# Sums of the second feed-forward's weights formed during the mixer and kept in DRAM

## The chip, the core and the metric

The kernel runs on one core of one Trainium2 chip. A core has TensorE (matmuls; PE in the profile, its weight loads PEld), VectorE (DVE), ScalarE (ACT), GpSimd (POOL) and SyncE (SP), which here only issues transfers. Transfers run on 16 DMA engines; each issuing engine has its queues, and SP's and POOL's carry nearly all bytes here. The metric is the device time of one execution in microseconds; lower is better.

## The reference, cut to what matters

One decoder layer for 256 tokens of width 2048 in float32: a feed-forward, a mixer (sliding-window attention beside an RWKV-7 recurrence, both gated), a cross-attention into 256 memory rows, a second feed-forward and a last norm.

```
def swiglu(h, w_gate, w_up, w_down):
    return (jax.nn.silu(h @ w_gate) * (h @ w_up)) @ w_down

x = x + 0.5 * swiglu(rms_norm(x, ffn1_norm), ffn1_w_gate, ffn1_w_up, ffn1_w_down)
x = gated_parallel_mixer(x, ...)        # w_in, w_proj_attn, w_proj_rwkv, w_out
x = memory_cross_attention(x, mem, ...) # w_cross_q, w_cross_kv, w_cross_o
x = x + 0.5 * swiglu(rms_norm(x, ffn2_norm), ffn2_w_gate, ffn2_w_up, ffn2_w_down)
return rms_norm(x, final_norm)
```

Each feed-forward has gate and up of 2048 x 5632 and a down of 5632 x 2048.

## The kernel before, in words

**Precision.** Each float32 operand is split into two fp32r parts, hi (a rounding, cast by ScalarE, L339) and lo (the rest, a subtraction on VectorE, L340). A product is three matmuls into one accumulator, xhi by hi, xhi by lo and xlo by hi (`times`, L413 to L415), each 128 x 128 by 128 x 512.

**Weights.** All weights stream from DRAM once, in the order of `weight_plan`. A unit is two chunks of 128 rows by 512 columns (KU = 2; 512 KB). `load` issues it on SP's queue into a ring: in the feed-forwards two units as one transfer of 1 MB into "raw2" (4 buffers of 1 MB), otherwise 512 KB into "raw" (4 buffers). `split_unit` makes hi and lo, in rings of three. `next_item` hands the next unit (or pair of units) to the products and keeps loads four units ahead and splits two units ahead. SP takes its transfers in order: a load that waits for its buffer holds all behind it. In the mixer a unit serves both blocks of 128 tokens: 12 matmuls.

**The feed-forward.** Its 11 blocks of 512 columns come in groups of 4, 4 and 3 (`GROUPS`). Block 0 takes gate and up one after the other by plain `product`; blocks 1 to 10 take them together by `product_pair`, over 8 chunk pairs q: two chunks of rows of both gate and up, with the two blocks of tokens. After each group comes a part of down, by `product_pair` too (but for the last two quarters of the last group).

**Pairs in seven.** A chunk pair is a product of a 2 x 2 block matrix of inputs by one of weights: eight products (24 matmuls). For the q in `SEVEN` it takes seven (21 matmuls) by Winograd's form of Strassen's scheme, p1 to p7, from sums of the input blocks (`combinations`, made once for all column blocks, in the feed-forward's beginning) and sums of the weight blocks. The weight sums are formed in place by `sums`: four VectorE subtractions of 128 x 512 (L350 to L353) from the raw gate and up rows into two "raw" buffers, then two casts (thi, L355) and two rests (tlo, L356) into one buffer each of four chunks. p1 to p7 stand in the order p1, p2, p7, p6, p4, p3, p5. Four accumulators of the scheme are finished at the last pair in seven of a block (`first` after p1, `middle` after p5). Gate and up have `SEVEN` = (0, 2, 4), so that a plain pair stands between two pairs in seven; down has (2, 4, 6) or (2, 4).

**The mixer and what fills it.** The plain products of the mixer run as a list, and small work is put between their units by `bg` (`Interleave`): groups of Python generators, one step at each tick; a tick is called after each row block of a unit, so two to a unit. A group has a limit of generators that run at once. `idle(n)` lets n ticks pass, and `bg.seen` holds the names of events. The attention stage has a loop n = 0 to 3 over the attention's gate columns and `w_proj_attn` (L1088); the RWKV part has `substitute` (31 steps of a triangular solve on VectorE) and a chain of small matmuls for each pair of heads; then come `w_proj_rwkv`, `w_out`, the cross-attention's weights, and the second feed-forward. POOL's queue moves rows that are put off to DRAM and fetched again (x1d, md, gl, ml, mem).

**What sets the order.** The program is written engine by engine in this interleaved order; a scheduler then orders each engine's instructions by what is ready, within what the buffers allow, so the built order may differ from the written one. `issue_after` puts an instruction behind another one.

## Time and profile before

| | us |
|---|---|
| median of three runs | 2270.05 (2268.65 to 2270.73) |
| the profiled execution | 2267.66 |
| its span | 2265.9 |
| first feed-forward, about | 0 to 730 |
| mixer and cross-attention, about | 730 to 1556 |
| second feed-forward, about | 1556 to 2253 |

The span is the time from the first to the last instruction of the profiled execution; the difference to its time, 1.8 us, lies around it. A row of a group of instructions gives the line, the engine, the operation, output<-inputs, partitions x elements and type, count, then busy microseconds, mean nanoseconds of one, and the idle time just before them with what ended it. A row of the timeline gives start, duration, engine, line and operation, and in brackets the idle time before it and what ended that. A row of windows gives the stretch, its length, the busy time and count of each engine, the granted TensorE clock (1.00 is full), the DMA engines' busy share and GB/s. A row of transfers gives output<-input, queue, count, KB each and the median time from issue to landing; the names of rings ("raw", "hi", "acc") are the tags above. Matmuls overlap, so their durations add up to more than the time that they take.

### The profile page before, as it was taken

Reading aid. Unit: us, or ns where it says so; the run is one execution under the profiler, and the core shown is the slowest. Engines: PE = TensorE matmul, PEld = TensorE weight load, DVE = VectorE, ACT = ScalarE, POOL = GpSimd, SP = SyncE. Lnnn points to the kernel's source line nnn. Section 1 sums busy time; section 2 is a strip of 40 time slices with the busy share of each in tenths; the row PEclk is TensorE's granted clock in tenths of the full one; section 3 lists DMA queues with packets and bytes.
Section 4 is the critical chain, followed back from the end, with each engine's and each line's share of the span. In section 5 each row is a group of like instructions: output and inputs, shape, how many; then the busy total and the mean of one; then the engine's idle time right before and its main releaser. Section 6 shows DMA issues by size and latency. Waiting matters only on the chain.

```text
span 2265.9 us, 28100 instructions
## 1 busy us (share of the span) xinstructions
PE 2244.2 (99%) x10613; PEld 1840.5 (81%) x10613; DVE 1784.2 (79%) x2283; ACT 1230.7 (54%) x1655; POOL 134.1 (6%) x194
## 2 busy tenths in 40 slices
PE   9999999999999999999999999999999999999998
PEld 7888888888888877788888888888888888888886
DVE  7899989898988477895444556547899998998987
ACT  6555555555556477544444446556555555555554
POOL 1000000000001000201220021001000000000001
PEclk9999999999999999999999999999999999999999
DMA  7565565555556544676533486657555556556563
GB/s 262 186 206 200 189 212 196 186 204 205 187 195 203 164 134 140 195 229 208 150 88 93 154 262 228 195 168 262 202 187 205 203 198 210 186 188 220 186 212 141
DMA packets 219240, 432.75 MB, mean 191 GB/s; under 512 B 14140, under 2 KB 16417, under 8 KB 219105
## 3 DMA queue, kind: packets, MB, share of 16 engines
q1 hardware_dynamic: 210432, 404.78, 54.1%
q0 software_dynamic: 8208, 25.39, 3.5%
q8 instruction: 83, 1.36, 0.2%
q10 hardware_dynamic: 464, 0.79, 0.1%
q14 instruction: 53, 0.43, 0.1%
HBM read 417.56 MB, written 13.11 MB: 190 GB/s over the span
## 4 chain that ended last, share of the span: by engine, by line
PE 86%; DVE 5%; issue 4%; DMA 2%; ACT 2%; POOL 0%; SPq 0%; POOLq 0%; DVEq 0%; ACTq 0%
PE acc L413 17%; PE acc L414 17%; PE acc L415 17%; PE mm L414 7%; PE mm L415 7%; PE mm L413 7%; DVE lo L340 2%; PE tr L600 2%; PE tr L414 2%; PE tr L415 2%; PE tr L413 2%; PE mm L1212 1%; DMA raw<-in_ffn_w_down_dram 1%; PE tr L1181 1%; ACT hi L339 1%
## 5 line engine op out<-in xcount | busy, mean ns | idle before, releaser
L339 ACT CAST hi<-raw 128x1024 fp32r<-128x1024 f32 (+1 forms) x770 | 766.0, 997 | 731.1 <-PE acc L415 423.8
L340 DVE TENSOR_TENSOR lo<-raw,hi 128x1024 fp32r<-128x1024 f32 (+1 forms) x770 | 892.2, 1164 | 341.5 <-ACT hi L339 339.5
L413 PE MATMUL acc<-hi,xhi 128*128 128x512 f32 (+1 forms) x1196 | 476.9, 399 | 3.1 <-ACT xhi L627 2.5
L414 PE MATMUL acc<-lo,xhi 128*128 128x512 f32 (+1 forms) x1196 | 465.8, 389 | 2.2 <-DVE lo L340 2.0
L415 PE MATMUL acc<-hi,xlo 128*128 128x512 f32 (+1 forms) x1196 | 464.6, 389 | 0.0
L413 PEld LDWEIGHTS acc<-hi,xhi 128*128 128x128 f32 x1196 | 224.7, 188 | 52.5 <-issue 5.1
L414 PEld LDWEIGHTS acc<-lo,xhi 128*128 128x128 f32 x1196 | 224.9, 188 | 49.9 <-DVE lo L340 4.4
L415 PEld LDWEIGHTS acc<-hi,xlo 128*128 128x128 f32 x1196 | 224.4, 188 | 47.6 <-DVE xlo L628 1.0
L355 ACT CAST thi<-raw 128x1024 fp32r<-128x1024 f32 x172 | 180.4, 1051 | 102.3 <-DVE raw L351 55.1
L356 DVE TENSOR_TENSOR tlo<-raw,thi 128x1024 fp32r<-128x1024 f32 x172 | 208.9, 1221 | 4.5 <-ACT thi L355 4.5
L413 PE MATMUL mm<-hi,xhi 128*128 128x512 f32 x380 | 149.2, 393 | 0.0
L415 PE MATMUL mm<-hi,xlo 128*128 128x512 f32 x380 | 148.1, 390 | 0.0
L414 PE MATMUL mm<-lo,xhi 128*128 128x512 f32 x380 | 148.1, 390 | 0.0
L414 PE MATMUL acc<-lo,hhi 128*128 128x512 f32 x372 | 145.5, 391 | 0.4 <-DVE lo L340 0.4
L415 PE MATMUL acc<-hi,hlo 128*128 128x512 f32 x372 | 145.4, 391 | 0.0
L413 PE MATMUL acc<-hi,hhi 128*128 128x512 f32 x372 | 145.1, 390 | 0.0
L415 PEld LDWEIGHTS mm<-hi,xlo 128*128 128x128 f32 x380 | 71.3, 188 | 15.0
L413 PEld LDWEIGHTS mm<-hi,xhi 128*128 128x128 f32 x380 | 71.4, 188 | 14.5
L414 PEld LDWEIGHTS mm<-lo,xhi 128*128 128x128 f32 x380 | 71.4, 188 | 14.5
L414 PEld LDWEIGHTS acc<-lo,hhi 128*128 128x128 f32 x372 | 69.9, 188 | 14.9 <-DVE lo L340 0.8
L350 DVE TENSOR_TENSOR raw<-raw,raw 128x512 f32<-128x512 f32 x86 | 59.1, 688 | 28.9 <-DMA raw<-in_ffn_w_up_dram 23.7
L413 PEld LDWEIGHTS acc<-hi,hhi 128*128 128x128 f32 x372 | 69.8, 188 | 14.4
(386 smaller groups left out, 3559.1 us busy)
## 6 DMA issues: line engine op xcount, KB each, us to landing
raw<-in_ffn_w_up_dram SPq DMA_DIRECT2D x88, 1024.0 KB, 6.8
raw<-in_ffn_w_down_dram SPq DMA_DIRECT2D x88, 1024.0 KB, 5.5
raw<-in_ffn_w_gate_dram SPq DMA_DIRECT2D x84, 1024.0 KB, 5.3
raw<-in_w_in_dram SPq DMA_DIRECT2D x136, 512.0 KB, 3.8
raw<-in_w_out_dram SPq DMA_DIRECT2D x32, 512.0 KB, 4.7
raw<-in_w_proj_attn_dram SPq DMA_DIRECT2D x16, 512.0 KB, 3.6
raw<-in_w_proj_rwkv_dram SPq DMA_DIRECT2D x16, 512.0 KB, 5.7
raw<-in_w_cross_kv_dram SPq DMA_DIRECT2D x16, 512.0 KB, 3.7
```

Source lines behind the costliest of these rows:

```text
L339: at["hi"] = act.copy(hi[:, s], raw[:, s])
L340: at["lo"] = dve.tensor_tensor(lo[:, s], raw[:, s], f32(hi[:, s]), ALU.subtract)
L350: dve.tensor_tensor(ta[:, 0], ru[:, 0], rg[:, 0], ALU.subtract)
L355: act.copy(hi[:, 2 * i : 2 * i + 2], t[:])
L356: dve.tensor_tensor(lo[:, 2 * i : 2 * i + 2], t[:], f32(hi[:, 2 * i : 2 * i + 2]), ALU.subtract)
L413: pe.matmul(o, xh, hi, start=first, stop=False, **how)
L414: pe.matmul(o, xh, lo, start=False, stop=False, **how)
L415: pe.matmul(o, xl, hi, start=False, stop=last, **how)
L600: pe.transpose(b[:, o : o + P], tok[:, t, col : col + P], ident[:])
L1181: pe.matmul(b[e][:, m * P : (m + 1) * P], x1[r, j, cs_], x2[r, j, cs_], start=True, stop=True,)
L1212: pe.matmul(vb[:, o : o + P][:, r], lhs(e), rhs[:, r], start=first and e == 0, stop=True, **ek,)
```

## The change

Only the second feed-forward (`last`) gets other pairs: gate and up take seven products for q = 0 to 4 (`SEVEN_2`), down for q = 2 and 4 (`SEVEN_DOWN_2`); the first keeps its pairs. Of the five, the weight sums of q = 0, 1, 3 and 4 (`STAGED`) in ten column blocks, 40 items, are not formed in place. A generator `stage`, spawned in a bg group of its own at the mixer's beginning, forms them: it loads gate's and up's two chunks (512 KB each, SP's queue) into one tile "stage" of four chunks, lets four ticks pass, subtracts four times on VectorE, and stores the tile (1 MB, SP's queue) to `sums_d` in DRAM. Six items are made early; the rest after the event "stage", at n = 2 of the loop over the attention's gates.

In the second feed-forward `load_sums` reads the sums of a staged item in two transfers of 512 KB into the ring "raw", issued on SP's queue after the weight loads; the up weights' first chunk of such a pair, which only the sums need, is not loaded any more (`first_unused`). q = 2 still forms its sums in place.

Two things change in both feed-forwards. The buffers thi and tlo of four chunks become thia, tloa, thib and tlob of two, one of each, with other sums together in a half. And the order of the seven products is p7, p6, p1, p2, p3, p4, p5: the sums' products come first.

```diff
 GROUPS = ((0, 4), (4, 4), (8, 3))
 N4 = 20
+STAGE_EARLY = 6
 AHEAD, LOADED = 2, 4
 SEVEN, SEVEN_DOWN = (0, 2, 4), ((2, 4, 6), (2, 4))
+SEVEN_2, SEVEN_DOWN_2 = (0, 1, 2, 3, 4), ((2, 4), (2, 4))
+STAGED = (0, 1, 3, 4)
 class Act:
@@ -85,13 +90,14 @@
                 for w in (wg, wu):
                     yield w, 0, KD, 0, 512
             else:
-                yield (wg, wu), 0, KD, (j * 512, j * 512), SEVEN
-        yield (wd, wd), 4 * j0, 4 * nj, (0, 512), SEVEN_DOWN[nj < 4]
+                yield (wg, wu), 0, KD, (j * 512, j * 512), SEVEN_2 if last else SEVEN
+        seven = SEVEN_DOWN_2 if last else SEVEN_DOWN
+        yield (wd, wd), 4 * j0, 4 * nj, (0, 512), seven[nj < 4]
         if last and (j0, nj) == GROUPS[-1]:
             for n in (2, 3):
                 yield wd, 4 * j0, 4 * nj, n * 512, 512
         else:
-            yield (wd, wd), 4 * j0, 4 * nj, (1024, 1536), SEVEN_DOWN[1]
+            yield (wd, wd), 4 * j0, 4 * nj, (1024, 1536), seven[1]
 def weight_plan(a):
@@ -148,6 +154,7 @@
     bg.group("chain", 3)
     bg.group("norm", 1)
     bg.group("mem", 1)
+    bg.group("stage", 1)
     def f32(x):
         return x.bitcast(F32)
@@ -294,7 +301,7 @@
-    plan, units, items, ends = [], [], [], []
+    plan, units, items, ends, staged = [], [], [], [], {}
     for entry in weight_plan(a):
         if entry is None:
             ends.append(len(units))
@@ -309,8 +316,14 @@
         for k in range(k0, k0 + nk, 2 * KU):
             u = len(units)
             units += [(v, k + i, c, 512) for v, c in zip(w, c0) for i in (0, KU)]
-            items += [((u + i, u + 2 + i), (k - k0) // KU + i in n) for i in range(2)]
-    raws, parts = {}, {}
+            for i in range(2):
+                q = (k - k0) // KU + i
+                if n == SEVEN_2 and q in STAGED:
+                    staged[len(items)] = len(staged)
+                items.append(((u + i, u + 2 + i), q in n))
+    raws, parts, summed = {}, {}, {}
+    first_unused = {items[i][0][1] for i in staged}
+    sums_d = dram.tile([len(staged), P, 4, 512], F32, name="sums")
     at = {"item": 0, "product": 0, "pool": None}
     def load(u, pieces=None):
@@ -326,9 +339,51 @@
             raw = wp.tile([P, KU, n], F32, tag="raw", name="raw", bufs=4)
         for i in range(m):
             raws[u + i] = raw[:, i * KU : (i + 1) * KU, :]
+        if u in first_unused:
+            second = u + 1 in first_unused
+            pieces = [(slice(1, 2), nc.sync)] + [(slice(2 + second, 4), nc.sync)]
+            if not second:
+                pieces = ((slice(1, 4), nc.sync),)
+        elif u + 1 in first_unused and wide:
+            pieces = ((slice(0, 2), nc.sync), (slice(3, 4), nc.sync))
         for i, queue in pieces or ((slice(0, m * KU), nc.sync),):
             rows = slice((k + i.start) * P, (k + i.stop) * P)
             queue.dma_start(raw[:, i], w[rows, c0 : c0 + n].rearrange("(a p) n -> p a n", p=P))
+    def load_sums(i):
+        if i not in staged or i in summed:
+            return
+        summed[i] = [
+            wp.tile([P, KU, 512], F32, tag="raw", name="raw", bufs=4) for _ in range(2)
+        ]
+        for e, t in enumerate(summed[i]):
+            nc.sync.dma_start(t[:], sums_d[staged[i], :, KU * e : KU * e + KU, :])
+    def stage(sp):
+        for i, n in staged.items():
+            if n == STAGE_EARLY:
+                yield from wait_for("stage")
+            t = sp.tile([P, 4, 512], F32, tag="stage", name="stage")
+            g, u = (units[v] for v in items[i][0])
+            for e, (w, k, c0, _) in ((2, g), (0, u)):
+                rows = slice(k * P, (k + KU) * P)
+                nc.sync.dma_start(
+                    t[:, e : e + KU], w[rows, c0 : c0 + 512].rearrange("(a p) n -> p a n", p=P)
+                )
+            yield from idle(4)
+            u0, u1, g0, g1 = (t[:, e] for e in range(4))
+            with tc.issue_after(at["lo"].ins):
+                dve.tensor_tensor(g0, u0, g0, ALU.subtract)
+                dve.tensor_tensor(u0, u1, u0, ALU.subtract)
+            yield
+            with tc.issue_after(at["lo"].ins):
+                dve.tensor_tensor(u1, u1, g0, ALU.subtract)
+                dve.tensor_tensor(g1, g1, u1, ALU.subtract)
+            yield from idle(2)
+            nc.sync.dma_start(sums_d[n], t[:])
+            yield from idle(2)
     def split_unit(u, rows=slice(0, KU)):
         n, raw = units[u][3], raws[u]
@@ -340,23 +395,24 @@
             at["lo"] = dve.tensor_tensor(lo[:, s], raw[:, s], f32(hi[:, s]), ALU.subtract)
         return hi, lo
-    def sums(g, u):
-        sp, rg, ru = at["pool"], raws[g], raws[u]
-        ta, tb = (wp.tile([P, KU, 512], F32, tag="raw", name="raw", bufs=4) for _ in range(2))
-        hi = sp.tile([P, 4, 512], F32R, tag="thi", name="thi")
-        lo = sp.tile([P, 4, 512], F32R, tag="tlo", name="tlo")
-        dve.tensor_tensor(ta[:, 0], ru[:, 0], rg[:, 0], ALU.subtract)
-        dve.tensor_tensor(ta[:, 1], ru[:, 1], ru[:, 0], ALU.subtract)
-        dve.tensor_tensor(tb[:, 0], ru[:, 1], ta[:, 0], ALU.subtract)
-        dve.tensor_tensor(tb[:, 1], rg[:, 1], tb[:, 0], ALU.subtract)
-        for i, t in enumerate((ta, tb)):
-            act.copy(hi[:, 2 * i : 2 * i + 2], t[:])
-            dve.tensor_tensor(
-                lo[:, 2 * i : 2 * i + 2], t[:], f32(hi[:, 2 * i : 2 * i + 2]), ALU.subtract
-            )
-        return hi, lo
+    def sums(g, u, t=None):
+        sp, out = at["pool"], []
+        if t is None:
+            rg, ru = raws[g], raws[u]
+            t = [wp.tile([P, KU, 512], F32, tag="raw", name="raw", bufs=4) for _ in range(2)]
+            dve.tensor_tensor(t[1][:, 0], ru[:, 0], rg[:, 0], ALU.subtract)
+            dve.tensor_tensor(t[0][:, 0], ru[:, 1], ru[:, 0], ALU.subtract)
+            dve.tensor_tensor(t[0][:, 1], ru[:, 1], t[1][:, 0], ALU.subtract)
+            dve.tensor_tensor(t[1][:, 1], rg[:, 1], t[0][:, 1], ALU.subtract)
+        for e, v in zip("ab", t):
+            hi = sp.tile([P, KU, 512], F32R, tag="thi" + e, name="thi")
+            lo = sp.tile([P, KU, 512], F32R, tag="tlo" + e, name="tlo")
+            act.copy(hi[:], v[:])
+            dve.tensor_tensor(lo[:], v[:], f32(hi[:]), ALU.subtract)
+            out.append((hi, lo))
+        return out
     def divide(i):
         if i >= len(items) or i in parts:
@@ -367,7 +423,7 @@
             return
         g, u = which
         if seven:
-            parts[i] = split_unit(g), split_unit(u, slice(1, 2)), sums(g, u)
+            parts[i] = split_unit(g), split_unit(u, slice(1, 2)), sums(g, u, summed.get(i))
         else:
             parts[i] = split_unit(g), split_unit(u)
@@ -385,7 +441,9 @@
                 break
             for v in items[j][0]:
                 load(v)
+            load_sums(j)
             divide(j)
+        load_sums(i + 2)
         return parts[i]
     def product(x: Act, w, skew=False):
@@ -422,12 +480,12 @@
                 k + i == 0, k + i == nk - 1,
             )
-    def combinations(sp, x: Act, seven, name, ready=lambda: True, early=True):
+    def combinations(sp, x: Act, seven, name, ready=lambda: True, early=True, n=0):
         pairs = [q for q in range(max(seven) + 1) if early or q in seven]
-        n = 12 if not early else sum(4 if q in seven else 2 for q in pairs)
+        n = n or sum(4 if q in seven else 2 for q in pairs)
         parts = [sp.tile([P, n, P], F32R, tag=name + e, name=name + e) for e in ("hi", "lo")]
         c = {"parts": parts, "at": {}, "done": False, "seven": seven, "early": early}
@@ -505,16 +563,17 @@
                 bg.until(lambda: c["done"] and (q > min(seven) or not bg.groups["feat"][1]))
                 g, u, s = next_item()
                 end = q == max(seven)
+                ta, tb = s
                 for i, (to, x_, w_) in enumerate((
+                    ("p7", of_c(q, 2), of_w(ta, 0)), ("p6", of_c(q, 1), of_w(ta, 1)),
                     ("p1", of_x(0, k), of_w(g, 0)), ("p2", of_x(0, k + 1), of_w(g, 1)),
-                    ("p7", of_c(q, 2), of_w(s, 1)), ("p6", of_c(q, 1), of_w(s, 2)),
-                    ("p4", of_x(1, k + 1), of_w(s, 3)), ("p3", of_c(q, 3), of_w(u, 1)),
-                    ("p5", of_c(q, 0), of_w(s, 0)),
+                    ("p3", of_c(q, 3), of_w(u, 1)), ("p4", of_x(1, k + 1), of_w(tb, 1)),
+                    ("p5", of_c(q, 0), of_w(tb, 0)),
                 )):
                     add(to, x_, w_, end and to in ("p1", "p5", "p6", "p7"))
                     if i % 2:
                         bg.tick()
-                    if end and i == 1:
+                    if end and to == "p1":
                         first(b)
                 if end:
                     middle(b)
@@ -654,21 +713,23 @@
         if last:
             for tag, shape, dt, bufs in (
                 ("hhi", [P, 16, T], F32R, 1), ("hlo", [P, 16, T], F32R, 1),
-                ("hb", [P, 2, 512], F32, 2), ("thi", [P, 4, 512], F32R, 1),
-                ("tlo", [P, 4, 512], F32R, 1),
+                ("hb", [P, 2, 512], F32, 2), ("thia", [P, KU, 512], F32R, 1),
+                ("tloa", [P, KU, 512], F32R, 1), ("thib", [P, KU, 512], F32R, 1),
+                ("tlob", [P, KU, 512], F32R, 1),
             ):
                 sp.tile(shape, dt, tag=tag, name=tag, bufs=bufs)
         begun = at["item"]
         c = combinations(
-            sp, norm.x, SEVEN, "c", lambda: norm.r is not None and at["item"] > begun + 4
+            sp, norm.x, SEVEN_2 if last else SEVEN, "c", lambda: norm.r is not None and at["item"] > begun + 4
         )
         c["next"] = []
+        seven = SEVEN_DOWN_2 if last else SEVEN_DOWN
         for gi, (j0, nj) in enumerate(GROUPS):
             h = Act(
                 [sp.tile([P, 16, T], F32R, tag="hhi", name="hhi")],
                 [sp.tile([P, 16, T], F32R, tag="hlo", name="hlo")], 16,
             )
-            ch = combinations(sp, h, SEVEN_DOWN[nj < 4], "d", early=False)
+            ch = combinations(sp, h, seven[nj < 4], "d", early=False, n=4 * len(seven[0]))
             def transposed(hb, c):
                 for q in range(2):
@@ -766,6 +827,7 @@
     with tc.tile_pool(name="mx", bufs=1, reuse_waits="tile") as sp:
         aligned(sp)
         abias, mask3, mask_l, bdones, bdmean, keep = mixer_constants(sp)
+        bg.spawn("stage", stage(sp))
         def t4(name, shape=(P, 4, T), dt=F32):
             return sp.tile(list(shape), dt, tag="t4", name=name, bufs=N4)
@@ -1086,6 +1148,8 @@
         for n in range(4):
+            if n == 2:
+                bg.seen.add("stage")
             pg = product(n2.x, W["w_in"])
             g = t4("ga", (P, 2, 512))
             for t in range(2):
```

## The prediction

> **What bounds the kernel now.** I read the page's busy times and its chain first, then stretches of time, then TensorE's single instructions, because a busy share of matmuls that overlap says little.
>
> ```profile
> span 2265.9 us, 28100 instructions
> PE 2244.2 (99%) x10613; PEld 1840.5 (81%) x10613; DVE 1784.2 (79%) x2283; ACT 1230.7 (54%) x1655; POOL 134.1 (6%) x194
> DMA packets 219240, 432.75 MB, mean 191 GB/s; under 512 B 14140, under 2 KB 16417, under 8 KB 219105
> HBM read 417.56 MB, written 13.11 MB: 190 GB/s over the span
> PE 86%; DVE 5%; issue 4%; DMA 2%; ACT 2%; POOL 0%; SPq 0%; POOLq 0%; DVEq 0%; ACTq 0%
> ```
> ```profile
> 1699.86 0.39 PE L413 MATMUL acc<-hi,xhi 128*128 128x512 f32 x1
> ...
> 1710.52 0.39 PE L415 MATMUL acc<-hi,xlo 128*128 128x512 f32 x1
> ```
> ```profile
> core 0: us, PE busy (x) PEld busy (x) DVE busy (x) ACT busy (x) POOL busy (x), PEclk, DMA share, GB/s
> 964.00:1022.00 58.00, 57.03 (x250) 46.47 (x249) 54.31 (x85) 24.68 (x25) 0.73 (x1) 1.00 0.71 226
> ...
> 1372.00:1376.00 4.00, 4.00 (x19) 3.30 (x19) 1.30 (x2) 1.19 (x2) 0.00 (x0) 1.00 1.04 386
> ...
> 1300.00:1420.00 120.00, 120.00 (x568) 99.05 (x567) 73.71 (x87) 65.05 (x99) 23.87 (x24) 1.00 0.74 244
> 1420.00:1530.00 110.00, 110.00 (x509) 90.40 (x508) 57.56 (x70) 57.28 (x85) 1.31 (x2) 1.00 0.58 183
> 1556.00:2253.00 697.00, 696.61 (x3116) 574.87 (x3115) 624.66 (x770) 385.56 (x444) 16.39 (x16) 1.00 0.58 200
> ```
>
> The two matmul rows are the first and the last of 48 that follow each other: (1710.52 - 1699.86) / 47 = 0.2268 us from start to start, though one lasts 0.39. So a 128x512 matmul less is worth 0.227 us, not 0.39. The second feed-forward (1556 to 2253) needs 3,042 such matmuls by the code, 690 us of its 697; the 88 transposes of hb are most of the rest. TensorE sets its length and is nearly gapless, at a granted clock of 1.00. VectorE is busy 624.66 of 697 there, and has room in the mixer. The transfers run at 200 GB/s in the feed-forward; the same 16 engines moved 386 in the best four microseconds.
>
> **The change part by part.**
>
> *Fewer products.* A chunk pair of plain form takes 24 matmuls, one in seven 21. Ten column blocks get two more such pairs: 10 x 2 x 3 = 60 matmuls fewer. The first down product of the groups of four loses its third: 2 x 3 = 6 more. Net 54 x 0.2268 = -12.2 us. Nothing hides it: it is TensorE's own time. It is also the most that the change can bring.
>
> *The engines beside it.*
>
> ```profile
> L340 DVE TENSOR_TENSOR lo<-raw,hi 128x1024 fp32r<-128x1024 f32 x220 | 270.5, 1238 | 48.6 <-ACT hi L339 48.1
> L356 DVE TENSOR_TENSOR tlo<-raw,thi 128x1024 fp32r<-128x1024 f32 x84 | 102.0, 1221 | 2.2 <-ACT thi L355 2.2
> L350 DVE TENSOR_TENSOR raw<-raw,raw 128x512 f32<-128x512 f32 x42 | 28.9, 688 | 15.3 <-DMA raw<-in_ffn_w_up_dram 12.4 <-DMA raw<-in_ffn_w_down_dram 2.8
> ...
> L340 DVE TENSOR_TENSOR lo<-raw,hi 128x512 fp32r<-128x512 f32 x42 | 28.8, 685 | 0.0
> ```
> ```profile
> L339 ACT CAST hi<-raw 128x1024 fp32r<-128x1024 f32 x220 | 230.8, 1052 | 210.2 <-PE mm L415 112.1 <-PE acc L415 77.4 <-issue 12.3
> L355 ACT CAST thi<-raw 128x1024 fp32r<-128x1024 f32 x84 | 88.1, 1051 | 50.4 <-DVE raw L351 27.0 <-DVE raw L353 23.1
> L339 ACT CAST hi<-raw 128x512 fp32r<-128x512 f32 x42 | 26.0, 618 | 20.3 <-PE acc L415 17.5 <-ACT thi L355 2.7
> ```
>
> In the feed-forward 20 more pairs need two tlo each and half a lo less: 20 x (2 x 1.22 - 0.55) = +38 us of VectorE. Sums formed in place fall from 30 to 10 in gate and up, and by 2 in down: -22 x 4 x 0.688 = -60. Two fewer pairs in down save 4. VectorE ends near 600 of 685, ScalarE near 415: neither is a bound on average.
>
> *Five such pairs in a row, with one buffer of each half sum.* Before, a plain pair of 5.44 us lay between them. A pair now lasts 21 x 0.2268 = 4.76. Take the third, counted from the start of the second, in the order in which the ACT queue has it. Its up cast waits for the gate buffer, free after the 12th matmul (11 x 0.227 + 0.39 = 2.9), ends at 3.5; the next gate's cast waits for the 15th (3.6), ends at 4.6; thi's follows, 5.7; tlo, behind lo on VectorE, 6.95. Taken in the written order TensorE could begin the pair at 6.95 - 0.23 = 6.7, two late. The fourth loses the same, the fifth 0.9, the second 0.4 by the same steps: 5.3 us a block, 53 in all. But the built program does not keep that order. It lists TensorE's hi products of p7 and p6 early, and fills the gap with the products that are ready (p1 and p2 of the next pair, p4 and p5 of the last): such breaks in the order go from 48 to 202. With that list the same steps give a wait of about 0.2 us a block. Bounds 2 and 53 over ten blocks; I take +2, since the list is what runs.
>
> *The sums read back.* 40 x 1.05 MB more, 40 x 0.26 MB not loaded: a block reads 11.5 MB in about 41 us, 282 GB/s, under the 386. The loads wait for raw buffers that tlo frees, and SP holds the weight loads behind them in order.
>
> ```profile
> raw<-in_ffn_w_up_dram SPq DMA_DIRECT2D x88, 1024.0 KB, 6.8
> raw<-in_ffn_w_gate_dram SPq DMA_DIRECT2D x84, 1024.0 KB, 5.3
> raw<-in_w_in_dram SPq DMA_DIRECT2D x136, 512.0 KB, 3.8
> ...
> x1d<-x POOLq DMA_DIRECT2D x4, 512.0 KB, 4.4
> ```
>
> A half sum (512 KB) behind one 1 MB load lands in some 6.8 us; the fourth pair's are issued some 8 us before their cast. Taken as hidden; up to 1 us a block if it is not, 10 in all.
>
> *FFN1's order.* Its pairs in seven now start with p7 and p6, which need the sums, not with the gate's halves: wanted two products (1.36 us) earlier. The list of TensorE keeps the old rhythm in most blocks and breaks at the changes to down. Bounds 0 and 6 places x 1.36 = 8; I take +0.5, because the sums of a first pair are cast during the plain pairs ahead of it.
>
> *Forming the sums in the mixer.* 40 times: two loads, four subtractions (4 x 0.688 = 2.75 us), a store; 110 us of VectorE in some 800. On SP the store waits for VectorE and the next load for the store's landing, since there is one stage tile; the mixer's weight loads queue behind both, and VectorE's subtractions wait for the load with every lo behind them. So the cycle must fit.
>
> ```profile
> DMA packets 7487, 17.01 MB, mean 283 GB/s; under 512 B 528, under 2 KB 528, under 8 KB 7484
> ...
> raw<-in_w_out_dram SPq DMA_DIRECT2D x13, 512.0 KB, 6.0
> raw<-in_w_proj_rwkv_dram SPq DMA_DIRECT2D x7, 512.0 KB, 7.1
> ```
> ```profile
> raw<-in_w_cross_kv_dram SPq DMA_DIRECT2D x14, 512.0 KB, 3.7
> ```
> ```profile
> 1031.52 1.23 DVE L340 TENSOR_TENSOR lo<-raw,hi 128x1024 fp32r<-128x1024 f32 x1 [1.50 <-ACT hi L339]
> 1034.24 1.23 DVE L340 TENSOR_TENSOR lo<-raw,hi 128x1024 fp32r<-128x1024 f32 x1 [1.49 <-ACT hi L339]
> ```
>
> The first of these fences is the transfer view of 1320 to 1380, the second of 1420 to 1500. A unit of weights takes 12 x 0.2268 = 2.72 us of TensorE, as the two lo rows show, and VectorE idles 1.5 of it. In the built order a cycle of the stage spans six units in plain stretches, 16.3 us. It needs 5.3 (store) + 5.3 (load) + 0.4 + 2.75 + one lo of 1.23 = 15.0: it fits, by 1.3. VectorE runs some 3 us ahead of TensorE, which evens out single late ones.
>
> It does not fit from 1320 to 1380: the POOL queue moves its rows then, and 512 KB took 6.0 to 7.1 us, not 3.7. With 2.3 to 3.4 more on each leg the cycle is 19.6 to 21.8, 3.3 to 5.5 too long, over 60 / 16.3 = 3.7 cycles: 12 to 20 us. By bytes: 386 - 283 = 103 GB/s spare is 6.2 MB in 60 us, the stage wants 3.7 x 2.1 = 7.8; the rest takes 4 us, less what VectorE is ahead. So 1 to 20; I take +2, nearer the count of bytes, as the legs slow down only while the other queue is active.
>
> The Trainium skill, "DMA: Bandwidth & Descriptors", section "Bandwidth", speaks against this part: HBM to SBUF is bound near 358 GB/s for a core. By it 75 GB/s are spare, 4.5 MB, and the missing 3.3 MB take 9 us, not 4; the row of 386 says that this limit does not hold for a core alone, and the measurement decides. The same page, section "Anatomy of one DMA", warns that completion can be surprisingly long when the target is HBM (said of POOL's path); here 512 KB to DRAM took 4.4 against 3.8 to load, 0.6 more, and 40 cycles of 15.6 would still fit in 16.3.
>
> *The 31 steps of the substitution* (964 to 1022) fill VectorE: 54.31 of 58. Four of the 40 now lie in them, 11 us. The built order stretches the steps over 28 units instead of 21: 76.2 us for 54.3 + 11 + 7 x 1.23 + 1.4 = 75.3. Bounds 0 and 11; I take +1.
>
> Sum: -12.2 + 2 + 0.5 + 2 + 1 = -6.7. The profiled execution took 2267.66 (2265.9 of span and 1.8 around it) and would take 2260.9; the median of the three runs, 2270.05, lies 2.4 above it: 2263.3.
>
> **The rivals.**
>
> *The stage's cycle is late in the mixer (slower).* Place: the store, landing and load legs on SP, with VectorE's subtractions. For it: one tile, two in-order queues, landings of 6.0 to 7.1 us. Against it: 1.3 us of room elsewhere. At 20 us in the busy stretch, in place of 2, plus some cycles elsewhere: 2263.3 + 18 = 2281. It decides once it costs over 6.7 + 2 = 8.7 us.
>
> *Pairs in a row stall TensorE (slower).* For it: the thin slack above, one buffer per half. Half of the 53 us is 27, not 2: 2263.3 + 25 = 2288. It turns the sign from 0.9 us a block.
>
> *The waits eat the gain (no change).* Stalls of 8 to 17 us in all, from several of the terms at half their upper bounds: 2266 to 2274.
>
> *All of it arrives.* No stall at all: 2270.05 - 12.2 = 2257.8, the lower end.
>
> **How the numbers follow.** Faster by over 0.2% (below 2265.5; about what a measurement can tell from no change) 0.45, the forecast with its own range 2257.8 to 2265.5. Within 0.2%: 0.17. Late stage 0.23, stalled pairs 0.15, both slower: 0.38. The range reaches from 2257.5, the whole gain, to 2285, between the two slow cases, with about 0.1 left out above.
>
> **What would show it.** Right: TensorE with 54 matmuls fewer; some 84 MB more moved in the mixer, HBM written near 55 MB, total near 548; the second feed-forward 10 to 12 us shorter; the mixer at most 4 longer; 0.227 between matmuls also from the first to the fifth pair of a block. Wrong: VectorE's stage subtraction or ScalarE's thi waiting for a transfer, TensorE for tlo in every block, SP for the store of the sums over 2 us a cycle, w_out loads over 10 us to landing, or gaps where the feed-forward groups change to down. The whole is wrong if the mixer grows by more than the feed-forward shrinks.

## The result and the profile after

The changed kernel takes 2338.86 us (2334.30 to 2339.18), the kernel before in the same comparison 2269.35 (2267.51 to 2270.73): a ratio of 1.0302, with an interval of 1.0284 to 1.0320. The forecast was 2263.3; its range ended at 2285. The profiled execution took 2338.91, with a span of 2337.2. These are the rows of the page after that answer to those shown of before (span, busy times, bytes, chain).

```profile
span 2337.2 us, 28587 instructions
PE 2269.0 (97%) x10559; PEld 1841.7 (79%) x10559; DVE 1859.4 (80%) x2385; ACT 1260.1 (54%) x1689; POOL 136.1 (6%) x194
DMA packets 253484, 548.14 MB, mean 235 GB/s; under 512 B 17660, under 2 KB 19937, under 8 KB 248225
HBM read 490.96 MB, written 55.05 MB: 234 GB/s over the span
PE 64%; DMA 19%; DVE 10%; issue 3%; ACT 3%; SPq 1%; DVEq 0%; ACTq 0%; POOLq 0%; POOL 0%
PE acc L471 12%; PE acc L473 11%; PE acc L472 11%; DMA stage<-in_ffn_w_up_dram 6%; PE mm L473 6%; PE mm L472 6%; PE mm L471 6%; DMA sums<-stage 6%; DVE lo L395 3%; DMA raw<-sums 3%; PE tr L472 2%; PE tr L471 2%; PE tr L473 2%; PE tr L659 1%; DVE tlo L413 1%
```

The counts are as forecast: 54 matmuls fewer (10613 to 10559), 548 MB moved, 55 written. The chain is not: transfers had 2% of it and have 19%, the stage's load and store 6% each.

Where the time went is read from instructions that both kernels have. Three of VectorE's, before (first fence) and after (second): the mixer's first sum of squares, the second half of the second feed-forward's block 0, and the kernel's last scaling.

```profile
730.92 0.15 DVE L646 TENSOR_REDUCE ms<-ss 128x2 f32<-128x8 f32 x1
1600.25 0.75 DVE L690 SCALAR_TENSOR_TENSOR hb<-acc,rs,hb 128x512 f32<-128x512 f32 x1
2260.35 0.74 DVE L1475 SCALAR_TENSOR_TENSOR x<-x,rs,raw 128x512 f32<-128x512 f32 x1
```
```profile
732.79 0.15 DVE L705 TENSOR_REDUCE ms<-ss 128x2 f32<-128x8 f32 x1
1672.52 0.75 DVE L751 SCALAR_TENSOR_TENSOR hb<-acc,rs,hb 128x512 f32<-128x512 f32 x1
2331.85 0.75 DVE L1539 SCALAR_TENSOR_TENSOR x<-x,rs,raw 128x512 f32<-128x512 f32 x1
```

The changed kernel is 1.9 us late at the first, 72.3 at the second, 71.5 at the third. So the mixer (with cross-attention and block 0 of the feed-forward, which has no pairs in seven) lost 70.4 us, and the ten blocks that were to gain 12.2 gained 0.8. Two things are to be explained, and the same three instructions serve for every kernel below: "mixer" is the lateness gained from the first to the second, "feed-forward" from the second to the third, each against the profiled execution of before.

*The mixer.* The chain of the changed kernel from 1384 to 1411, in order of time (start, us, what), passes through one item of the stage:

```profile
1383.91 6.43 DMA sums<-stage
1390.33 0.02 issue
1390.35 0.37 SPq L372
1390.72 0.05 issue
1390.77 9.59 DMA stage<-in_ffn_w_up_dram
...
1400.48 0.06 DVE stage L378
1400.54 0.55 issue
1401.09 1.22 DVE lo L395
1402.31 0.60 DVE stage L379
...
1403.43 0.68 DVE stage L382
...
1404.77 0.80 PE acc L471
```

The store lands after 6.43 us, the load is issued at once and lands after 9.59, VectorE subtracts, with a lo part between, and TensorE waits at the end. The waits of SP's queue and of VectorE from 740 to 1620 say the same (us in total, times, longest):

```profile
SPq L372 <- DMA sums<-stage: 86.9, 32, 5.8
SPq L385 <- DVE stage L383: 53.6, 21, 7.0
```
```profile
L378 DVE TENSOR_TENSOR stage<-stage 128x512 f32<-128x512 f32 x39 | 26.9, 690 | 69.3 <-DMA stage<-in_ffn_w_up_dram 66.0 <-issue 3.2
```

VectorE stood for 66 us in front of its first subtraction, with the mixer's lo parts behind it. Since one tile holds the sums, store, landing, load and subtraction form a closed loop, and the in-order lists of SP and VectorE tie to each turn of it the weights that lie between (some six units in plain stretches). The stores of the 7th and of the 40th item:

```profile
983.96 0.34 SPq L385 DMA_DIRECT2D sums<-stage  x1
...
1619.88 0.34 SPq L385 DMA_DIRECT2D sums<-stage  x1
```

33 turns in 635.9 us are 19.3 each. Means over their rows: 6.1 from the store to the next load's issue, 0.4 between the two loads' issues, 8.1 from the second load's issue to the first subtraction, 4.6 to the end of the fourth. Over the same turns the kernel falls 60.5 us further behind (start of the same 128x512 matmul, counted through, in both kernels), so the work of before that is tied to a turn takes 17.4 us, 1.8 less than the loop. These means hide five different stretches:

| from, to (changed kernel) | turns | us a turn | work of before in it | falls behind by |
|---|---|---|---|---|
| 984 to 1111 | 7 | 18.1 | 17.4 | 4.5 |
| 1111 to 1146, where the chain of the RWKV heads begins | 2 | 17.6 | 11.1 | 12.9 |
| 1146 to 1318, that chain | 8 | 21.6 | 21.5 | 0.6 |
| 1318 to 1429, POOL's rows and w_out | 5 | 22.1 | 17.1 | 24.8 |
| 1429 to 1620 | 11 | 17.4 | 15.8 | 17.7 |

So the loss is uneven: 1.2 us a turn in the eighteen plain turns (first and last row), 6.4 in two where a turn spans little work, 5.0 in the five where POOL moves its rows (its store leg takes 7.2 us there, its load leg 9.6), and nothing in the eight that span 21.5 us of work each. Two shared VectorE instructions around those five turns, before and after, are 25.4 and 50.3 us late:

```profile
1286.39 0.68 DVE L1286 TENSOR_TENSOR yq<-yq,sq 128x512 f32<-128x512 f32 x1
...
1380.49 1.28 DVE L1354 TENSOR_TENSOR x<-acc,x 128x512 f32<-128x512 f32 x2
```
```profile
1311.79 0.68 DVE L1350 TENSOR_TENSOR yq<-yq,sq 128x512 f32<-128x512 f32 x1
...
1430.78 1.28 DVE L1418 TENSOR_TENSOR x<-acc,x 128x512 f32<-128x512 f32 x2
```

### The profile page after: what moved, and what is told of

Its sections match the earlier page's. It is cut to its first block, busy times and chain, and to the rows that moved or that the text cites. A ratio compares the mean times of both kernels' runs of the same rounds, so it can differ in the third digit from the quotient of the medians.

```text
span 2337.2 us, 28587 instructions
## 1 busy us (share of the span) xinstructions
PE 2269.0 (97%) x10559; PEld 1841.7 (79%) x10559; DVE 1859.4 (80%) x2385; ACT 1260.1 (54%) x1689; POOL 136.1 (6%) x194
## 3 DMA queue, kind: packets, MB, share of 16 engines
q8 instruction: 83, 1.36, 0.2%
## 4 chain that ended last, share of the span: by engine, by line
PE 64%; DMA 19%; DVE 10%; issue 3%; ACT 3%; SPq 1%; DVEq 0%; ACTq 0%; POOLq 0%; POOL 0%
PE acc L471 12%; PE acc L473 11%; PE acc L472 11%; DMA stage<-in_ffn_w_up_dram 6%; PE mm L473 6%; PE mm L472 6%; PE mm L471 6%; DMA sums<-stage 6%; DVE lo L395 3%; DMA raw<-sums 3%; PE tr L472 2%; PE tr L471 2%; PE tr L473 2%; PE tr L659 1%; DVE tlo L413 1%
## 5 line engine op out<-in xcount | busy, mean ns | idle before, releaser
L394 ACT CAST hi<-raw 128x1024 fp32r<-128x1024 f32 (+1 forms) x770 | 753.6, 987 | 738.9 <-PE acc L473 482.7
L395 DVE TENSOR_TENSOR lo<-raw,hi 128x1024 fp32r<-128x1024 f32 (+1 forms) x770 | 881.4, 1152 | 255.2 <-ACT hi L394 252.8
L471 PE MATMUL acc<-hi,xhi 128*128 128x512 f32 (+1 forms) x1136 | 456.3, 402 | 3.9 <-DVE ga L1159 2.3
L472 PE MATMUL acc<-lo,xhi 128*128 128x512 f32 (+1 forms) x1136 | 445.5, 392 | 4.7 <-DVE lo L395 4.7
L473 PE MATMUL acc<-hi,xlo 128*128 128x512 f32 (+1 forms) x1136 | 443.6, 391 | 0.0
L413 DVE TENSOR_TENSOR tlo<-raw,thi 128x1024 fp32r<-128x1024 f32 x208 | 250.6, 1219 | 21.5 <-ACT thi L412 19.4
L412 ACT CAST thi<-raw 128x1024 fp32r<-128x1024 f32 x208 | 216.1, 1051 | 83.9 <-DVE raw L407 28.0
L473 PEld LDWEIGHTS acc<-hi,xlo 128*128 128x128 f32 x1136 | 214.4, 189 | 45.1 <-issue 1.4
L378 DVE TENSOR_TENSOR stage<-stage 128x512 f32<-128x512 f32 x40 | 27.6, 690 | 70.7 <-DMA stage<-in_ffn_w_up_dram 67.3
L473 PEld LDWEIGHTS acc<-hi,hlo 128*128 128x128 f32 x374 | 70.3, 188 | 14.1
L473 PEld LDWEIGHTS mm<-hi,xlo 128*128 128x128 f32 x360 | 67.6, 188 | 14.2
```

The source lines that it names most:

```text
L378: dve.tensor_tensor(g0, u0, g0, ALU.subtract)
L394: at["hi"] = act.copy(hi[:, s], raw[:, s])
L395: at["lo"] = dve.tensor_tensor(lo[:, s], raw[:, s], f32(hi[:, s]), ALU.subtract)
L412: act.copy(hi[:], v[:])
L413: dve.tensor_tensor(lo[:], v[:], f32(hi[:]), ALU.subtract)
L471: pe.matmul(o, xh, hi, start=first, stop=False, **how)
```

## The experiments

**What the feed-forward does alone.** Three kernels without the stage. e1_no_stage reads stand-ins for the sums, e7_no_read reads nothing in their place, and e6_stride_8k reads stand-ins whose rows lie as far apart as those of the sums.

```diff
# all three
-        bg.spawn("stage", stage(sp))
# e1_no_stage (e6_stride_8k: W["ffn1_w_down"]; e7_no_read: t is the raw rows, no transfer)
-            nc.sync.dma_start(t[:], sums_d[staged[i], :, KU * e : KU * e + KU, :])
+            nc.sync.dma_start(
+                t[:], W["ffn1_w_gate"][rows, c0 : c0 + 1024].rearrange("p (a n) -> p a n", a=KU)
+            )
```

> The stage is left out: nothing is loaded, subtracted or stored in the mixer, and the second feed-forward reads 512 KB pieces of the first gate weights in place of the sums (same count, size and queue; the values are not the sums). If the feed-forward's lost gain is the late reading of the sums itself, the mixer returns to its time before and the feed-forward still gains about 1 us: 2269.4 + 1.9 (first feed-forward) - 0.8 = 2270. If the feed-forward lost its gain to what the stage left behind (late start, queues), the 12.2 come back: 2259. If five pairs in seven in a row stall of themselves, 2270 as well, but then the casts of the sums do not wait for transfers.

> No stage, and nothing read back: in the second feed-forward the casts of the half sums take the gate's and the up's raw rows as they lie in the ring (the values are not the sums; all of the up rows are loaded again). Matmuls, casts and lo parts of five pairs in seven in a row stay as in the change. If the reading of the sums is what costs the feed-forward its gain: near the full 12.2, 2256 to 2259, against 2263 of e1_no_stage. If the five in a row stall of themselves, with one buffer for each half: 2262 to 2265, no better than e1_no_stage.

> As e1_no_stage (no stage; stand-ins are read for the sums), but the 512 KB stand-ins come from the first down weights, whose rows lie 8 KB apart as those of the sums do (those of the gate weights lie 22 KB apart); pieces of 4 KB in both. If the sums land late because of how they lie in DRAM: the second feed-forward's gain against before falls from 7 us to about 0, 2270. If it is because they were written in this run or lie in another memory: 2263 as e1_no_stage.

| | time, us | ratio to before | mixer | feed-forward |
|---|---|---|---|---|
| e1_no_stage | 2262.95 | 0.9979 (0.9970 to 0.9989) | +0.8 | -7.1 |
| e7_no_read | 2263.78 | 0.9981 (0.9971 to 0.9991) | +1.7 | -5.5 |
| e6_stride_8k | 2265.18 | 0.9988 (0.9979 to 0.9998) | +1.0 | -3.2 |

e1_no_stage lies between its forecasts, e7_no_read at its second. (The profiled execution of e1_no_stage was the fastest of ten, 2.4 us under its median; by the medians its feed-forward gained some 5.) Half of the matmuls' gain arrives, and no more without any reading: the five pairs in seven in a row cost 5 to 7 of the 12.2 by themselves. TensorE's starts agree: gaps beyond the pace of 0.2268 add up to 8 to 9 us in the two kernels and to 3 before. The changed kernel loses the rest by reading, and it seems to matter what is read: the kernels with the five pairs that read what the stage wrote have a feed-forward of +1.8 to -3.3 (the changed one -0.8), those that read stand-ins from the gate weights or nothing -5.5 to -7.1, and the one whose stand-ins have the sums' distance of 8 KB has -3.2, at the edge of the first group. Landing times of the pieces that are read, in the changed kernel, in e1_no_stage and in e6_stride_8k:

```profile
raw<-sums SPq DMA_DIRECT2D x80, 512.0 KB, 6.7
```
```profile
raw<-in_ffn_w_gate_dram SPq DMA_DIRECT2D x60, 512.0 KB, 6.0
```
```profile
raw<-in_ffn_w_down_dram SPq DMA_DIRECT2D x80, 512.0 KB, 6.4
```

The order is that of the gains (e7_no_read apart, which reads nothing), but the intervals of e1_no_stage and e6_stride_8k overlap: that the distance does it is suggested, not settled.

**Which leg of the loop costs the mixer its time.** One thing is taken out of the stage at a time.

```diff
# e2_no_sub: the four tensor_tensor of the stage are left out
# e9_small_sub: each of them on [:, :16]
# e5_no_store
-            nc.sync.dma_start(sums_d[n], t[:])
# e4b_two_tiles, and N4 = 18
-            t = sp.tile([P, 4, 512], F32, tag="stage", name="stage")
+            t = sp.tile([P, 4, 512], F32, tag="stage", name="stage", bufs=2)
```

> The four subtractions of each stage item are left out: what is loaded is stored unchanged, with the same transfers, tile and queue (the values read back are not the sums). Theory, VectorE's wait for the stage's load with the mixer's lo parts behind it (67 us in the trace): the mixer loses at most 20 us and the whole takes 2275 to 2290. Rival, bytes (the transfers at 300 GB/s slow the weights whoever waits): 2320 or more. Rival, SP's queue (weight loads behind the store that waits): the store now waits for the load directly, 2310 or more.

> The changed kernel with each of the stage's subtractions cut from 512 to 16 columns (the sums are then mostly raw weights): waits, order, tile, queues and bytes stay, VectorE's 110 us of work shrink to some 10. If the waits between SP, the transfers and VectorE make the loss: at least two thirds of it stay, 2315 or more. If VectorE's work makes it (lo parts late behind 2.75 us of subtractions a cycle): near e2_no_sub, 2280 to 2295.

> The stage loads and subtracts but stores nothing (the second feed-forward reads pieces of the first gate weights in place of the sums). 42 of 84 MB and the wait for the store's landing are gone. Theory, serial cycle: 2272 to 2290. Rival, bytes: half the cost stays, 2300 to 2310.

> Two stage tiles in place of one (and 18 in place of 20 of the mixer's 4 KB tiles, to make room): a load no longer waits for the landing of the store just before it. Theory, the serial cycle of one tile makes the load late for VectorE: the load is issued some 5 us earlier, VectorE's wait falls from 67 to under 20 us, the whole takes 2275 to 2300. Rival, VectorE's wait is from the loads' own length (6.3 to 9.6 us against four ticks, 5.4 us), whatever the store does: 2310 or more, the wait still over 40.

Single executions, beside a before of 2268 to 2269: e2_no_sub 2282.08 (mixer +14.2), e9_small_sub 2300.20 (+33.8), e5_no_store 2277.90 (+16.3), e4b_two_tiles 2310.33 (+43.0). (Two tiles need more room: with N4 = 19, e4_two_tiles, the mixer's buffers come to 139.1 KB a partition where 137.1 are left.) All bytes move in the first and 56 us of the loss are gone, so in the stretches where it moves them the bytes are not the bound: its transfers ran at 296 GB/s from 740 to 1300, the changed kernel's at 252 from 740 to 1620. But without subtractions its items come sooner, and the last is stored at 1289: it moves none in the time of POOL's rows, 1290 to 1420 of before. There the changed kernel loses 35 us, e9_small_sub 21, e4b_two_tiles 17 and e5_no_store, which also moves half the bytes, 6; no run separates the bytes from the loop in that stretch. Subtractions that take hardly any time but keep their waits leave half of the loss, 33.8 of 70.4: the forecast of two thirds missed, and VectorE's 2.75 us a turn weigh as a leg of the loop. Two tiles free VectorE wholly, as forecast, but only 27 us come back. The waits of e4b_two_tiles, SP's and then ScalarE's, tell why:

```profile
SPq L385 <- DVE stage L383: 143.6, 39, 6.3
SPq L372 <- DMA sums<-stage: 30.7, 12, 7.5
```
```profile
ACT hi L394 <- DMA raw<-in_w_in_dram: 66.9, 33, 6.8
ACT hi L394 <- DMA raw<-in_w_proj_rwkv_dram: 21.1, 10, 6.4
```

The wait has changed its queue. SP's list runs ahead of VectorE's; the store now stands on SP for the subtractions, the weight loads stand behind it, and ScalarE waits for weights instead of VectorE for the stage.

**Other queues for the stage.** All three transfers on POOL's queue; the subtractions too; and two tiles with the store alone on POOL, or with the store behind the next item's loads.

```diff
# e3_pool_queue, c1_all_pool: loads and store
-                nc.sync.dma_start(
+                nc.gpsimd.dma_start(
# c1_all_pool also
-                dve.tensor_tensor(g0, u0, g0, ALU.subtract)
+            pool.tensor_tensor(g0, u0, g0, ALU.subtract)
# e8_store_pool: e4b_two_tiles and
-            nc.sync.dma_start(sums_d[n], t[:])
+            nc.gpsimd.dma_start(sums_d[n], t[:])
```

> The stage's three transfers are issued on POOL's queue in place of SP's; bytes, tile and VectorE's subtractions stay. If the weight loads behind the stage's waits on SP are what starves ScalarE: 2275 to 2290. If VectorE's wait for the stage's load is (theory): the wait stays near 67 us or grows, since the cycle is as long, and the time is 2320 or more.

> The whole stage on GpSimd: transfers on POOL's queue and the four subtractions on POOL, so that neither VectorE nor SP ever waits for a stage transfer; 84 MB still move. Theory (VectorE's wait is nearly all of the mixer's loss): the mixer loses 0 to 12 us, the whole takes 2265 to 2280. Rival, the transfers themselves: over 2300. A new wait is possible: POOL's row moves of the mixer queue behind the stage.

> As e4b_two_tiles, but the store of the sums is issued on POOL's queue in place of SP's; the loads stay on SP. If SP's wait for VectorE's subtractions with the mixer's weight loads behind it is what took the place of VectorE's wait (143.6 us there): SP holds nothing for the stage any more, POOL waits instead, weights land in time, the mixer loses 5 to 15 us and the whole takes 2272 to 2285. Rival, the weights are late for VectorE's work or for the bytes: 2300 to 2312 as with e4b_two_tiles.

> All 40 items, with two stage tiles, and the store of an item issued after the loads of the next (some five ticks after its subtractions in place of two), from the first attention gate block on; 18 in place of 20 of the mixer's 4 KB tiles. Theory, two waits across queues that take each other's place (VectorE for the load behind the store's landing with one tile, SP for VectorE's subtractions with weight loads behind it with two): both go, SP waits under 30 us for the subtractions and VectorE under 15 for the stage's loads, the mixer loses 5 to 20 us, the whole 2270 to 2285. Rival, the bytes beside the weights: the waits go and weights still land late, 2300 or more.

e3_pool_queue took 2401.54: as forecast VectorE's wait grew, to 149.2 us from 740 to 1720. e8_store_pool took 2293.68 (mixer +28.7): moving the store off SP gives 14 us back against two tiles alone, less than forecast, since SP still stands 118 us for the store's landing before a load. c1_all_pool took 2486.98 (1.0945 to 1.0984 of before) and c2_pipelined 2324.30 (1.0224 to 1.0255); both forecasts fell. In c2_pipelined the built order moved the store up again, and SP waited 169.6 us for the subtractions. In c1_all_pool POOL's own work was late; two rows of its subtractions, and its waits, over the whole run:

```profile
L380 POOL TENSOR_TENSOR stage<-stage 128x512 f32<-128x512 f32 x40 | 65.0, 1626 | 2.9
...
L377 POOL TENSOR_TENSOR stage<-stage 128x512 f32<-128x512 f32 x40 | 54.2, 1356 | 195.4 <-DMA stage<-in_ffn_w_up_dram 190.6 <-DVE lo L393 4.8
L372 POOL DMA_DIRECT2D stage<-in_ffn_w_gate_dram x40 | 29.0, 725 | 164.4 <-DMA sums<-stage 153.8 <-issue 10.6
```

A subtraction takes 1.36 to 1.63 us there against 0.69 on VectorE. The Trainium skill, "GPSIMD Engine Reference", section "Engine selection", gives GpSimd as about twice slower for elementwise work on two inputs; the trace agrees. The 344 us of waits did more harm: the differences of neighbouring tokens that POOL forms for the RWKV part (`d`, L965) stood behind them, and VectorE waited for these for 97 us. An engine that is 6% busy is not free if something needs it in time.

**A loop with room.** Pairs 0, 2, 3 and 4, of which 3 and 4 are staged: 20 items, 24 matmuls fewer than before (-5.4 us). One tile and SP's queue, but longer pauses; then the same behind the attention gates; then at chosen places. c3_twenty and c4_twenty_pool have two tiles and the late store, on SP and on POOL.

```diff
-SEVEN_2, SEVEN_DOWN_2 = (0, 1, 2, 3, 4), ((2, 4), (2, 4))
-STAGED = (0, 1, 3, 4)
+SEVEN_2, SEVEN_DOWN_2 = (0, 2, 3, 4), ((2, 4), (2, 4))
+STAGED = (3, 4)
# c5_twenty_slow: idle(6), idle(4), idle(6) in place of 4, 2, 2; from n == 0 on
# c6_after_solve: idle(5), idle(3), idle(5); "stage" seen after the loop over n
```

> As c2_pipelined, but four pairs in seven, 0, 2, 3 and 4, of which only 3 and 4 are staged: 20 items at longer intervals. 24 fewer matmuls in place of 54: 60 saved become 30, the down part costs 6: -5.4 us. Theory: the mixer loses 2 to 8 us, the feed-forward gains 2 to 5: 2265 to 2275. If a cycle that has room costs nothing: 2264.

> As c3_twenty (20 items, two tiles, the store behind the next item's loads), but the store on POOL's queue. If SP's 25 us of waits for the subtractions and 20 for the landings made c3_twenty's loss: 2265 to 2272. If it is that the loads themselves stand in SP's queue ahead of weights: 2277 as c3_twenty.

> The change with one stage tile and the queues as they are, but four pairs in seven, 0, 2, 3 and 4, of which 3 and 4 are staged: 20 items from the first attention gate block on, and longer pauses (six, four and six ticks in place of four, two and two), so that a cycle spans eight to nine units of weights, 22 to 24 us, in place of six. Matmuls: 30 fewer in gate and up, 6 ... 12 more in down than the full change would not have; in all 24 fewer than before, -5.4. If the loss is that a cycle of 19.3 us is tied to 17.4 us of work: with 22 to 24 us of work it has slack, the mixer loses 0 to 8, the feed-forward gains 2 to 5, the whole 2264 to 2274. If the loss belongs to each item (VectorE's work, bytes): 20 x 1.7 = 34 less some 4, 2295 or more.

> As c5_twenty_slow (20 items, one tile), but the stage begins behind the attention gates, so that none of it lies in the 31 steps of the substitution, where VectorE is full; a cycle spans seven units of weights in plain stretches (19.1 us by 2.72 each) and more time in the chain of the RWKV heads. If the 5.6 us that c5_twenty_slow lost by 1124 come from VectorE's full stretch: they go, the late stretches cost 2 to 6, the feed-forward gains 4.5: 2264 to 2270. If a loop of 19.3 us decides alone: no slack in the plain stretches, 2270 to 2276.

> As c6_after_solve (20 items, one tile, pairs 0, 2, 3 and 4 with 3 and 4 staged), but the items are put where a cycle has room: four behind the attention gates, eight in the chain of the RWKV heads at shorter pauses (two ticks each), three in the projections, and five after the third quarter of w_out, so that nearly none lies beside POOL's row transfers in w_out, where c6_after_solve lost all of its 9.3 us. If the loss belongs to the places where the loop of a cycle is longer than the work it is tied to: the mixer loses 0 to 3, the feed-forward gains 4.5: 2263 to 2267, a little faster than before. If each item costs something anywhere: 2270 to 2274 as c5_twenty_slow and c6_after_solve.

| | time, us | ratio to before | mixer | feed-forward |
|---|---|---|---|---|
| c3_twenty | 2277.38 | 1.0044 (1.0027 to 1.0062) | +20.5 | -4.4 |
| c4_twenty_pool | 2278.52 | 1.0044 (1.0031 to 1.0057) | +14.0 | -4.3 |
| c5_twenty_slow | 2271.06 | 1.0017 (1.0008 to 1.0027) | +8.3 | -4.4 |
| c6_after_solve | 2272.78 | 1.0019 (1.0010 to 1.0028) | +9.6 | -4.3 |
| c8_gaps | 2281.05 | 1.0056 (1.0042 to 1.0069) | +17.9 | -4.5 |

(The profiled execution of c3_twenty took 2284.75, 7 us more than its median, so its mixer stands 7 too high: the store on POOL changed nothing, and the loads in SP's queue remain.) With room the loop costs 0.4 us an item in c5_twenty_slow, where it cost 1.8. In c5_twenty_slow VectorE no longer waits for the stage; SP's waits from 740 to 1620 are

```profile
SPq L372 <- DMA sums<-stage: 27.5, 17, 3.5
SPq L385 <- DVE stage L383: 25.4, 20, 3.3
```

Where the rest is lost shows in two shared instructions: a scaling of rt and the sum of squares behind w_out, in the kernel before, in c5_twenty_slow and in c6_after_solve.

```profile
1124.75 1.22 DVE L1112 SCALAR_TENSOR_TENSOR rt<-rt,ee 128x1024 f32<-128x1024 f32 x1
...
1419.38 0.15 DVE L646 TENSOR_REDUCE ms<-ss 128x2 f32<-128x8 f32 x1
```
```profile
1130.36 1.22 DVE L1176 SCALAR_TENSOR_TENSOR rt<-rt,ee 128x1024 f32<-128x1024 f32 x1
...
1427.26 0.15 DVE L705 TENSOR_REDUCE ms<-ss 128x2 f32<-128x8 f32 x1
```
```profile
1124.01 1.22 DVE L1174 SCALAR_TENSOR_TENSOR rt<-rt,ee 128x1024 f32<-128x1024 f32 x1
...
1428.64 0.15 DVE L705 TENSOR_REDUCE ms<-ss 128x2 f32<-128x8 f32 x1
```

c5_twenty_slow has items around the substitution and is 5.6 late by 1124.75; c6_after_solve has none there and is 0.7 early. By 1419.38 it is 9.3 late: all of its loss lies where POOL moves its rows and w_out is loaded. Its time is that of the rival named for it, a loop without slack in every plain stretch, but the rows between 1040 and 1345 show no such loss. c8_gaps was to show that items moved out of that place cost nothing. It lost about 15 of its 17.9 us between 1290 and 1354 of before, where four items still lay, and nothing behind; but the three items that c6_after_solve had between 1300 and 1345 had cost it nothing. The lengths suggest a reason, not shown: a turn there takes 20 to 24 us in both kernels, near the 22.1 of the changed one, and spans five to eight units of weights, 14 to 22 us of work by 2.72 each; in c5_twenty_slow, which loses 2 there, it spans eight or nine. The place counts, and so does how the built order falls there; these runs don't separate the two. No kernel here that makes the sums in the mixer beats the one before.

**Sums in place in place of staged ones.** The five pairs of the change, with 1 and 3 staged only (`STAGED = (1, 3)`), and the stage of c6_after_solve.

> As c6_after_solve, but with the change's five pairs in seven, 0 to 4, of which 1 and 3 are staged and 0, 2 and 4 form their sums in place: the full 54 matmuls less with half the items. VectorE needs some 662 of 685 us in the second feed-forward. If VectorE has room for it: the feed-forward gains 5 to 7 and the whole takes 2262 to 2268. If not, it stalls at every third sum in place: 2275 or more.

2278.27, a ratio of 1.0044 (1.0030 to 1.0057): the mixer +10.0, near c6_after_solve, the feed-forward +1.3. With VectorE forming three sums of five in place, the whole gain of 12.2 is lost to waits.

## Why the prediction was wrong, point by point

*Fewer products:* right in count, and in price as a ceiling. Four pairs with a gain of 5.4 bring 4.3 to 4.5 in the feed-forward; the third pair in seven that down gives up was rightly counted against it.

*Five in a row, +2 with bounds of 2 and 53:* mis-sized. e7_no_read and e1_no_stage show 5 to 7. The list of TensorE was rightly preferred to the written order; what it leaves is small and everywhere, gaps of 0.1 to 1.2 us.

*The sums read back, hidden, bounds 0 and 10:* wrong. Some 5 us, from -0.8 against -5.5 to -7.1. The landing of 6.8 us was right (6.7 measured), but the cover of 8 us was not kept everywhere: ScalarE's thi waited 19.0 us for the sums, 18 times.

*FFN1's order, +0.5:* 1.9 here, -0.6 to +1.0 in the other kernels with the same first feed-forward: nothing that could be told from zero.

*The substitution, +1 with bounds 0 and 11:* near, 2.8. The steps last 77.6 us in the changed kernel against 57.0 before, where the prediction had 76.2, and TensorE falls from 7.1 to 9.9 us late over them. c5_twenty_slow and c6_after_solve differ by 6 at 1124.75, of which some 2 lie ahead of the steps.

*The stage's cycle, +2 with bounds 1 and 20:* this is the step that failed, with most of the 70 us that the mixer lost, and it failed in two places.

Outside the busy stretch the prediction put the lateness at nothing: a cycle of 15.0 against 16.3 of work. The work was right, 16.4 in the eighteen plain turns. The cycle was not: it takes 17.7 there, 1.2 late a turn, 22 us, and two turns at the beginning of the heads' chain cost 13 more. The 15.0 took store and load at a landing time of 5.3, that of a transfer with little ahead of it. In the loop they are never alone: over all turns the store leg measures 6.1 and the load leg 8.1 (7.0 of it the landing, with weights ahead on the queue), and the subtractions take 4.6 with the lo parts among them. The prediction itself had the better number: for the sums read back it took 6.8 us "behind one 1 MB load". Put twice into the loop that gives 6.8 + 6.8 + 0.4 + 2.75 + 1.23 = 18.0, near the 17.7, and the room of 1.3 is gone. (That 40 times 18.0 - 16.3 is 68, near the whole loss, is chance: eight turns cost nothing, and seven cost 5 to 6 each.)

In the busy stretch the legs were right and the choice was wrong. They gave a cycle of 19.6 to 21.8 and 12 to 20 us; the trace has five turns of 22.1, and 24.8 us. The prediction took 2, by the count of bytes and because the legs slow down only for a while.

The rival "the stage's cycle is late in the mixer" named the place, the mechanism and the sign, and even the point from which it decides. Its 20 us were near what the busy stretch cost; what was missing is the rest, its "some cycles elsewhere".

*Bytes.* 103 GB/s to spare between 1320 and 1380 was the argument for choosing 2. The changed kernel's trace doesn't bear it out in that stretch: from 1318 to 1332 its DMA engines were busy all the time, at 388 GB/s, and over the five turns they were 0.88 busy at 314 GB/s, with dips in between. e2_no_sub, which showed room for the bytes elsewhere, moved none of them there, so how much of the 24.8 us is bytes and how much is waiting in the loop stays open. The Trainium skill, "DMA: Bandwidth & Descriptors", section "Specifications", bounds a core near 358 GB/s; in the changed kernel's transfer view from 1320 to 1380 slices of 1.5 us reach 410 and 426, so that figure was not the limit here.

## What to carry to other kernels

A loop over one buffer (load, compute, store, landing, load) has a length of its own, and in-order queues tie everything behind its waits to that length. Add up its legs with landing times taken under the load it will meet, from transfers that stand behind others on the same queue, and compare with the work between two turns; if the margin is smaller than the spread of these landings, assume every turn with so little work to be late, not only those where the transfers are busiest. A second buffer moved such a wait to the next in-order queue here and did not end it; longer intervals ended VectorE's wait for the loads.

## What the runs showed of the hardware that was not expected

TensorE's waits cost more than they last. After the item above, its timeline (start, duration) reads

```profile
1400.51 0.39 PE L471 MATMUL acc<-hi,mthi 128*128 128x512 f32 x1
1402.36 0.50 PE L472 MATMUL acc<-lo,mthi 128*128 128x512 f32 x1 [1.46 <-DVE lo L395]
1404.77 0.80 PE L471 MATMUL acc<-hi,mthi 128*128 128x512 f32 x1 [1.90 <-DVE gl L1397]
...
1406.21 0.63 PE L471 MATMUL acc<-hi,mthi 128*128 128x512 f32 x1
1406.64 0.63 PE L472 MATMUL acc<-lo,mthi 128*128 128x512 f32 x1
...
1410.48 0.63 PE L471 MATMUL acc<-hi,mthi 128*128 128x512 f32 x1
1410.91 0.43 PE L472 MATMUL acc<-lo,mthi 128*128 128x512 f32 x1
1411.17 0.40 PE L473 MATMUL acc<-hi,mtlo 128*128 128x512 f32 x1
```

Two waits within four microseconds, 3.36 in all, and matmuls then start 0.43 us apart instead of 0.227 until 1410.91; the granted clock from 1404 to 1411 is 0.51. Some 40 matmuls of the mixer run at that pace (42 last 0.63 us, none before): 0.2 us each, about 8 of the 70 us. The longest such stretch lasts from 1124 to 1145, at a clock of 0.50, where the heads' small matmuls are slow too; it begins within a wait of 5.58 us for a VectorE instruction that stood behind the stage's subtractions. The kernel's mean granted clock fell from 0.999 to 0.987. The Trainium skill, "TensorE: Matmul & The Clock Gate", section "What's actually happening", has the clock halved after an idle window of about 3.4 us and given back after as long a busy one; a halved clock agrees with the pace of 0.43, while here it lasted 6.1 us from the first slow matmul, with a wait no longer than 1.90 in one piece. The forecast priced waits at their length alone.
